# Fp16 halves for the values and probabilities of the second attention, with one more buffer for each pool and a new layout

## The chip, the cores and the metric

The kernel runs on one core of a Trainium2 chip, as one program from the input in DRAM to the output in DRAM. The time is in device microseconds. A core has five engines that run side by side and wait for each other through semaphores: TensorE (PE; its weight loads are listed apart as PEld), VectorE (DVE), ScalarE (ACT), GpSimd (POOL) and SyncE (SP), whose queue issues all transfers of this kernel. Each engine works through its instructions in order, so that an instruction that waits holds up everything behind it.

## What is computed

One block of a transformer on a sequence of 1024 positions of width 1024: a gated FFN at half weight, a mix of two attentions, a second FFN, and a last normalization.

```python
h = rmsnorm(x, ffn1_norm);  x = x + 0.5 * swiglu(h, w1, w3, w2)
h = rmsnorm(x, mix_norm);   x = x + token_mix(h, ...)
h = rmsnorm(x, ffn2_norm);  x = x + 0.5 * swiglu(h, ...)
return rmsnorm(x, final_norm)

# token_mix: proj = h @ w_in, split into the parts of both attentions
y_da  = diff_attention(q_da, k_da, v_da, ...)   # 8 heads: softmax(q1 k1) - lam * softmax(q2 k2), times v (128 wide)
# second attention, 16 heads in 2 groups of 8; a group shares keys and values of 64 columns
o_cmp = softmax(q @ kc) @ vc                    # kc, vc: 63 compressed blocks of keys and values
o_slc = softmax(qr @ ks, causal) @ vs           # top 16 of 16 blocks: every causal key
o_win = softmax(qr @ kw, last 512 keys) @ vw
y_ns  = g0 * o_cmp + g1 * o_slc + g2 * o_win
merged = sigmoid(g_a) * (y_da @ w_proj_da) + sigmoid(g_b) * (y_ns @ w_proj_nsa)
return merged @ w_out
```

Everything is in float32, and the kernel keeps near that accuracy by splitting an operand into a high and a low half and multiplying the halves apart.

## The kernel before

The span runs through these stages in turn: the first FFN (to about 700 us), projections and the compressed keys and values of the second attention (to about 970), the first attention (`da_phase`, with its own projections ahead, to about 1474), the second attention (`ns_phase`, 1474 to 2092), and the output products with the second FFN.

**The second attention.** Work goes head by head (`hd`, 16 of them, two of a pair for one `H`) and, within a head, over `m`, two blocks of 128 queries. `ns_scores` computes for each block the scores of the selected (`Ps`) and of the window branch (`Pw`): the matmuls on L886 (`S<-kt,qt`), the mask and maximum on DVE (L893), the exponential with its sum on ACT (L895), the normalization with the gate on POOL (L1052). `ns_pv` then multiplies probabilities and values of the block before. `tr_split` transposes up to four 128x128 pieces of probabilities into PSUM (L941, `tr`), and `split` makes two halves of them: ACT writes the high half `th` (L89), DVE the low half `tl` (L85). For each piece or pair of pieces two matmuls follow, with 128 or 256 columns, the values `vt` as the weights: `v` times `th` (L1098) and `v` times `tl` (L1099). The weights hold the values as high and low halves beside each other, 64 columns of each; `ns_fold` (L1107, L1108) adds the two halves of the result up. The compressed branch `pc` times `vc` opens each output tile (L1064). In between `fill.step` puts products of later stages (`gm`, L52 to L54, with weights `whi` and `wlo` from L1162 and L85) into the order of the engines.

**The first attention** has the same shape with its own lines (L963 to L965 for the three value products). Its `da_finish` copies the output (`ob`, L971) and squares it (`sq`, L973); `da_finish2` sums the squares with a matmul by ones (`tot`, L980), scales (`m`, L982), takes a reciprocal root (L155 to L160, on ACT and POOL), multiplies (L986) and splits into `yo` (L89, L85), which is stored (`syd`, L990).

**The values** of the second attention are made in `v_ns_unit`, in the stage of projections: a projection, transposes (`tr`, L671), the split into `vv` and a store per group into `s_v2` (`sv<-vv`, L675). `vv` has one buffer. `ns_load_values` reads them back as `vt`.

**What sets the order.** A scheduler places the instructions of each engine by priority, and a tile's buffers and address come from its pool in the order in which pools are opened. Pools of the second attention are laid over those of the first, so that a first write to a buffer waits for the last reader of what lay there before. SP issues its transfers in the order of its queue.

## Time and profile before

| | |
|---|---|
| median of 3 runs | 2930.38 us (2929.75 to 2931.03) |
| the profiled execution | 2929.13 us |
| its span, first to last instruction | 2927.3 us |
| mean granted clock of TensorE in the span | 0.989 |
| TensorE busy | 2813.9 us |
| DVE, ACT, POOL busy | 2003.0, 1364.6, 789.2 us |

The span is the time between the first and the last instruction of the core; 1.8 us of the profiled execution lie around it. Busy times are sums of an engine's instructions that count overlapping ones once. The granted clock is that of TensorE as a share of full speed. Times in the trace count from the span's start.

### The profile page before, as it was taken

To read this page: it belongs to the slowest core of one execution; us is meant where nothing else is said; L and a number is where in the kernel's file an instruction comes from. 1 tells how busy PE (TensorE), PEld (TensorE's weight loads), DVE (VectorE), ACT (ScalarE), POOL (GpSimd) and SP (SyncE) were. 2 spreads that over 40 slices of the span, in tenths; PEclk is the share of its full clock that TensorE was granted. 3 is DMA by queue.
4 is the path that set the end of the run, shared out by engine and by line. 5 is a ranking of instruction groups with operands and counts; after the bars stand their busy time and mean duration, and the time that the engine had idled before them with its cause. 6 is when DMAs were issued, how large, how long until landed. Compare 5 with 4: busy or idle time off the path is not lost. (4 is left out here: it accounts for less than half of the span.)

```text
span 2927.3 us, 40127 instructions
## 1 busy us (share of the span) xinstructions
PE 2813.9 (96%) x14276; PEld 2122.4 (73%) x14276; DVE 2003.0 (68%) x3347; ACT 1364.6 (47%) x2347; POOL 789.2 (27%) x701
## 2 busy tenths in 40 slices
PE   8999999999999899989989999999999999999998
PEld 6644447888788678778778988888888854444886
DVE  7876866666587467767767777777343876675666
ACT  7533424442333245445566666666332653343443
POOL 3133321000144123322233333333242414233001
PEclk9999999999999999999999999999999999999999
DMA  4355448655456545544432225222753246444854
GB/s 162 123 200 183 168 169 283 216 180 165 145 197 237 178 151 179 180 163 152 149 114 84 87 95 184 87 87 76 289 167 107 77 155 223 159 179 162 296 181 144
DMA packets 212713, 478.21 MB, mean 163 GB/s; under 512 B 20897, under 2 KB 39585, under 8 KB 212513
## 3 DMA queue, kind: packets, MB, share of 16 engines
q1 hardware_dynamic: 212512, 475.65, 47.6%
q8 instruction: 112, 1.84, 0.3%
q14 instruction: 89, 0.72, 0.1%
HBM read 313.56 MB, written 162.00 MB: 162 GB/s over the span
## 5 line engine op out<-in xcount | busy, mean ns | idle before, releaser
L405 PEld LDWEIGHTS <-w 128*128 128x128 f16 x3024 | 297.1, 99 | 381.9 <-issue 30.7
L52 PE MATMUL gm<-hi,whi 128*128 128x512 f32 x880 | 351.7, 400 | 4.2 <-ACT whi L89 1.8
L54 PE MATMUL gm<-hi,wlo 128*128 128x512 f32 x880 | 347.9, 396 | 1.1 <-DVE wlo L85 1.1
L53 PE MATMUL gm<-lo,whi 128*128 128x512 f32 x880 | 348.0, 395 | 0.0
L405 PE MATMUL Y<-tf,w 128*128 128x512 f16 x1296 | 296.3, 383 | 20.7 <-DVE u L443 16.9
L85 DVE TENSOR_TENSOR tl<-tr,th 128x512 fp32r<-128x512 f32 (+2 forms) x384 | 233.1, 619 | 86.3 <-ACT th L89 74.9
L886 PE MATMUL S<-kt,qt 128*128 128x320 f32 (+5 forms) x1152 | 264.0, 348 | 26.3 <-ACT Pt L895 9.6
L89 ACT ACTIVATE th<-tr 128x512 fp32r<-128x512 f32 (+2 forms) x384 | 201.5, 543 | 182.0 <-PE tr L941 172.6
L85 DVE TENSOR_TENSOR wlo<-st,whi 128x1024 fp32r<-128x1024 f32 x154 | 197.5, 1300 | 113.8 <-ACT whi L89 112.6
L893 DVE CUSTOM_DVE_ANT_0 S<-S,slab 128x896 f32<-128x896 f32 (+7 forms) x320 | 224.0, 710 | 50.3 <-PE S L886 45.1
L53 PE MATMUL acc<-wlo,whi 128*128 128x512 f32 (+1 forms) x628 | 244.1, 389 | 1.0 <-DVE wlo L85 1.0
L89 ACT ACTIVATE whi<-st 128x1024 fp32r<-128x1024 f32 x154 | 160.6, 1057 | 178.5 <-PE acc L54 107.3
L54 PE MATMUL acc<-whi,wlo 128*128 128x512 f32 (+1 forms) x628 | 242.8, 389 | 0.0
L52 PE MATMUL acc<-whi 128*128 128x512 f32 (+1 forms) x628 | 240.3, 387 | 0.0
L886 PEld LDWEIGHTS S<-kt,qt 128*128 128x128 f32 x1152 | 184.5, 190 | 43.6 <-ACT Pt L895 11.4
L1052 POOL TENSOR_SCALAR Ps<-Ps,l 128x384 f32<-128x384 f32 (+7 forms) x128 | 98.5, 770 | 404.9 <-DVE l L1050 236.9
L405 PE MATMUL X<-h,w 128*128 128x512 f16 x864 | 195.3, 379 | 0.5 <-ACT s L415 0.5
L52 PEld LDWEIGHTS gm<-hi,whi 128*128 128x128 f32 x880 | 168.0, 191 | 37.5 <-ACT whi L89 2.8
L54 PEld LDWEIGHTS gm<-hi,wlo 128*128 128x128 f32 x880 | 167.7, 191 | 37.4 <-DVE wlo L85 1.8
L53 PEld LDWEIGHTS gm<-lo,whi 128*128 128x128 f32 x880 | 168.0, 191 | 30.7
L85 DVE TENSOR_TENSOR wlo<-wst,whi 128x1024 fp32r<-128x1024 f32 x103 | 138.7, 1348 | 54.6 <-ACT whi L89 44.5
L1099 PE MATMUL o<-tl,vt 128*128 128x256 f32 (+1 forms) x608 | 159.3, 294 | 15.3 <-DVE tl L85 15.1
(320 smaller groups left out, 6123.0 us busy)
## 6 DMA issues: line engine op xcount, KB each, us to landing
wst<-in_win_dram SPq DMA_DIRECT2D x55, 512.0 KB
sw<-w2s SPq DMA_DIRECT2D x44, 512.0 KB
st<-sw SPq DMA_DIRECT2D x88, 256.0 KB
st<-saT SPq DMA_DIRECT2D x88, 256.0 KB
a<-in_f1w_dram SPq DMA_DIRECT2D x36, 512.0 KB
a<-in_f2w_dram SPq DMA_DIRECT2D x36, 512.0 KB
st<-saB SPq DMA_DIRECT2D x66, 256.0 KB
qt<-sq SPq DMA_DIRECT2D x128, 128.0 KB
```

Source lines behind the costliest of these rows:

```text
L52: first = nc.tensor.matmul(out, lhsT=w[0][:, wk], rhs=x[0], start=start, stop=False, skip_group_check=skip)
L53: nc.tensor.matmul(out, lhsT=w[0][:, wk], rhs=x[1], start=False, stop=False, skip_group_check=skip)
L54: nc.tensor.matmul(out, lhsT=w[1][:, wk], rhs=x[0], start=False, stop=stop, skip_group_check=skip)
L85: return nc.vector.tensor_tensor(out=lo, in0=src, in1=hi.bitcast(F32), op=ALU.subtract)
L89: nc.scalar.activation(out=hi, in_=src, func=AF.Copy)
L405: K.mark = nc.tensor.matmul(o, lhsT=w[:, a, m * h + k], rhs=x[k][:, b], start=start and k == 0 and i == 0, stop=k == h - 1 and i == 2, ski ...
L886: K.last = nc.tensor.matmul(S[:, o:o + n], lhsT=q, rhs=k[:, k0 + c:k0 + c + n], start=i == 0, stop=i == 1)
L893: nc.vector.tensor_tensor_reduce(out=sv, in0=sv, in1=mv, scale=-0.125, scalar=BIG, op0=ALU.add, op1=ALU.min, accum_out=nm)
L1052: nc.gpsimd.tensor_scalar(out=p[:, 0:n], in0=p[:, 0:n], scalar1=l[:, c:c + 1], scalar2=1.0, op0=ALU.mult, op1=ALU.mult)
L1099: nc.tensor.matmul(dst, lhsT=v, rhs=lo[:, b * P:(b + n) * P], start=False, stop=last, skip_group_check=True)
```

## The change

The values of the second attention and its transposed probabilities are held as two halves of fp16 instead of float32. For that `v_ns_unit` only copies the transposed values to `vraw` and adds up their squares; the new `ns_value_scale` derives one power of two from the sum, scales all values by it, splits them into fp16 halves and stores them. The probabilities are multiplied by 2^14 where POOL normalizes them, the compressed values by both factors, and `ns_fold` divides by both. `np`, the pool of probabilities, has 6 buffers instead of 5, and `nt`, that of `th` and `tl`, 4 instead of 3. The pools of `ns_phase` are opened in another order, with queries and `pc` in two pools of one buffer each; the first queries and the first `pc` are loaded ahead of `wslab`. `da_finish2` of the last head is placed under another priority.

```diff
@@ v_ns_unit
-        vv = K.mq.tile([P, 2, 4, 2, 64], F32R, tag="vv", name="vv")
+        nc.vector.tensor_copy(out=K.vraw[br][:, tb * 4:tb * 4 + 4], in_=tr)
+        jk = K.mq.tile([P, TB], BF16, tag="vj", name="vj")
+        nc.scalar.activation(out=jk, in_=tr.rearrange("p j d -> p (j d)"), func=AF.Square,
+                             accum_out=K.vss[:, br * 2 + tb:br * 2 + tb + 1])
+
+
+def ns_value_scale(K):
+    nc = K.nc
+    one = K.mq.tile([P, 1], F32, tag="vone", name="vone")
+    nc.vector.tensor_reduce(out=one, in_=K.vss, axis=AX.X, op=ALU.add)
+    tot = K.gm.tile([P, TB], F32, tag="gm", name="tot")[:, 0:1]
+    nc.tensor.matmul(tot, lhsT=K.ones, rhs=one, start=True, stop=True)
+    s, v = pow2_scale(K, K.cst, tot, 51)
+    K.vscale = K.cst.tile([P, 2], F32, name="vscale")
+    nc.vector.tensor_scalar(out=K.vscale[:, 0:1], in0=s, scalar1=P_NS, scalar2=None, op0=ALU.mult)
+    nc.vector.tensor_scalar(out=K.vscale[:, 1:2], in0=v, scalar1=1.0 / P_NS, scalar2=None, op0=ALU.mult)
+    for br in range(2):
         for g in range(2):
-            split(nc, vv[:, g, :, 0], vv[:, g, :, 1], tr[:, :, g * 64:(g + 1) * 64])
-            nc.sync.dma_start(out=K.s_v2[br][g][:, tb * 4:tb * 4 + 4],
-                              in_=vv[:, g].rearrange("p j a d -> p j (a d)").bitcast(F32))
+            src = K.vraw[br][:, :, g * 64:(g + 1) * 64]
+            t = K.mq.tile([P, 8, 2, 64], F16, tag="vv", name="vv")
+            nc.scalar.activation(out=t[:, :, 0], in_=src, func=AF.Copy, scale=s)
+            nc.vector.scalar_tensor_tensor(out=t[:, :, 1], in0=src, scalar=s, in1=t[:, :, 0], op0=ALU.mult, op1=ALU.subtract)
+            nc.sync.dma_start(out=K.s_v2[br][g], in_=t.rearrange("p j a d -> p j (a d)"))
...
@@ tr_split
-    hi = K.tp.tile([P, TB], F32R, tag="th", name="th")
-    lo = K.tp.tile([P, TB], F32R, tag="tl", name="tl")
-    split(nc, hi[:, 0:n], lo[:, 0:n], tr[:, 0:n])
+    dt = F16 if K.narrow else F32R
+    hi = K.tp.tile([P, TB], dt, tag="th", name="th")
+    lo = K.tp.tile([P, TB], dt, tag="tl", name="tl")
+    if K.narrow:
+        nc.scalar.activation(out=hi[:, 0:n], in_=tr[:, 0:n], func=AF.Copy)
+        nc.vector.tensor_tensor(out=lo[:, 0:n], in0=tr[:, 0:n], in1=hi[:, 0:n], op=ALU.subtract)
...
@@ ns_scores
+        p1 = K.pp.tile([P, 5 * P], F32, tag="P1", name="Pw")
         p0 = K.pp.tile([P, T], F32, tag="P0", name="Ps")
-        p1 = K.pp.tile([P, 5 * P], F32, tag="P1", name="Pw")
...
-            nc.gpsimd.tensor_scalar(out=p[:, 0:n], in0=p[:, 0:n], scalar1=l[:, c:c + 1], scalar2=1.0,
+            nc.gpsimd.tensor_scalar(out=p[:, 0:n], in0=p[:, 0:n], scalar1=l[:, c:c + 1], scalar2=P_NS,
@@ ns_pv
+            if hd + m == 0:
+                order_after(K, first, K.last)
@@ ns_fold
-    nc.scalar.activation(out=y[mine], in_=o[other], func=AF.Copy)
-    nc.vector.tensor_tensor(out=y[mine], in0=o[mine], in1=y[mine], op=ALU.add)
+    nc.scalar.activation(out=y[mine], in_=o[other], func=AF.Copy, scale=K.vscale[other, 1:2])
+    nc.vector.scalar_tensor_tensor(out=y[mine], in0=o[mine], scalar=K.vscale[mine, 1:2], in1=y[mine], op0=ALU.mult, op1=ALU.add)
@@ constants
-B_NP = 5
+B_NP = 6
-B_NT = 3
+B_NT = 4
@@ da_phase
-        da_finish2(K, *K.fin)
+        with K.tc.high_priority(offset=-100):
+            da_finish2(K, *K.fin)
@@ ns_phase
+        K.qp, K.pcp = [open_pool(K, ctx, "nq0", 1)], [open_pool(K, ctx, "npc0", 1)]
+        q0 = ns_queries(K, 0, 0)
+        pc0 = ns_compressed(K, 0, 0)
         K.wslab = open_pool(K, ctx, "wsl", 1).tile([P, 5 * P], F32, name="wslab")
         nc.sync.dma_start(out=K.wslab, in_=K.A["wslab"])
-        K.qp, K.kp, K.pcp = open_pool(K, ctx, "nq", 2), open_pool(K, ctx, "nk", 1), open_pool(K, ctx, "npc", B_NPC)
-        K.pp, K.sm, K.tp, K.op = (open_pool(K, ctx, "np", B_NP), open_pool(K, ctx, "nsm", 6), open_pool(K, ctx, "nt", B_NT),
+        K.kp = open_pool(K, ctx, "nk", 1)
+        K.pcp.append(open_pool(K, ctx, "npc1", 1))
+        K.qp.append(open_pool(K, ctx, "nq1", 1))
+        K.tp, K.sm, K.pp, K.op = (open_pool(K, ctx, "nt", B_NT), open_pool(K, ctx, "nsm", 6), open_pool(K, ctx, "np", B_NP),
```

Line numbers shift with the change: L886 becomes L909, L895 L918, L941 L964, L971 and L973 become L999 and L1001, L980 L1008, L1098 and L1099 become L1144 and L1145, L1162 becomes L1208.

On ACT, at the passage from the first attention to the second, before (the first rows are the last splits of the first attention, `ob` and `sq` its last finish, `Ps` and `Pw` the first exponentials of the second):

```order
L89 ACTIVATE th<-tr 128x384
L971 ACTIVATE ob<-o 128x512
L895 ACTIVATE Ps,l<-S,nm 128x128
L895 ACTIVATE Pw,l<-S,nm 128x128
L973 ACTIVATE sq<-ob 128x512
L1162 ACTIVATE whi<-wst 128x1024
L895 ACTIVATE Ps,l<-S,nm 128x256
L895 ACTIVATE Pw,l<-S,nm 128x256
L895 ACTIVATE Ps,l<-S,nm 128x384
L155 ACTIVATE yr<-m 128x512
```

and after:

```order
L89 ACTIVATE th<-tr 128x384
L999 ACTIVATE ob<-o 128x512
L1001 ACTIVATE sq<-ob 128x512
L155 ACTIVATE yr<-m 128x512
L156 ACTIVATE yr<-yr 128x512
L157 ACTIVATE zr<-yr 128x512
L89 ACTIVATE yo<-ob 128x512
L918 ACTIVATE Ps,l<-S,nm 128x128
L918 ACTIVATE Pw,l<-S,nm 128x128
L918 ACTIVATE Ps,l<-S,nm 128x256
```

The steps of the finish, from `sq` to `yo`, have moved ahead of the first exponential.

On TensorE at the same place, from the last value product of the first attention on, before:

```order
L965 MATMUL o<-th,vt 128x128
L886 MATMUL S<-kt,qt 128x256 x2
L52 MATMUL gm<-hi,whi 128x512
L53 MATMUL gm<-lo,whi 128x512
L54 MATMUL gm<-hi,wlo 128x512
L52 MATMUL gm<-hi,whi 128x512
L53 MATMUL gm<-lo,whi 128x512
L54 MATMUL gm<-hi,wlo 128x512
L886 MATMUL S<-kt,qt 128x384 x2
L980 MATMUL tot<-sq,ones 128x512
```

and after:

```order
L993 MATMUL o<-th,vt 128x128
L1008 MATMUL tot<-sq,ones 128x512
L909 MATMUL S<-kt,qt 128x256 x2
L52 MATMUL gm<-hi,whi 128x512
L53 MATMUL gm<-lo,whi 128x512
L54 MATMUL gm<-hi,wlo 128x512
```

The finish's product by ones, `tot`, now stands first behind the value products.

On ACT in the stage of projections, behind the activation `gt` of the compressed keys, before (`vv` are the last two splits of the values, `kc` and `kbh` the compressed keys, `rh` a rotated projection, `whi` weights):

```order
L796 ACTIVATE gt<-gt 126x256
L89 ACTIVATE vv<-tr 128x4x64 x2
L809 ACTIVATE kc<-kcp 128x128
L812 ACTIVATE kbh<-kc 32x2x64 x4
L809 ACTIVATE kc<-kcp 128x128
L89 ACTIVATE whi<-wst 128x1024
L89 ACTIVATE rh<-m_6073 128x1024
```

and after:

```order
L817 ACTIVATE gt<-gt 126x256
L692 ACTIVATE vv<-vraw_5578,sc 128x8x64 x2
L692 ACTIVATE vv<-vraw_5579,sc 128x8x64 x2
L830 ACTIVATE kc<-kcp 128x128
L833 ACTIVATE kbh<-kc 32x2x64 x4
L830 ACTIVATE kc<-kcp 128x128
L89 ACTIVATE rh<-m_6092 128x1024
L89 ACTIVATE whi<-wst 128x1024
```

All four writes of `vv` stand here in a row now, and `rh` stands ahead of `whi`.

## Rows read from the trace of the kernel before

**Rows 1.** The page's busy times of the two busiest engines: busy us, share of the span, instructions.

```profile
PE 2813.9 (96%) x14276; PEld 2122.4 (73%) x14276; DVE 2003.0 (68%) x3347; ACT 1364.6 (47%) x2347; POOL 789.2 (27%) x701
```

**Rows 2.** Busy times by stretch of the span: window, its length, then the busy us (and instructions) of PE, PEld, DVE, ACT and POOL, the mean granted clock of TensorE, the share of the DMA engines, GB/s.

```profile
1453.00:1474.00 21.00, 16.77 (x90) 12.98 (x89) 10.17 (x18) 9.11 (x16) 4.85 (x4) 0.84 0.28 104
1474.00:1491.00 17.00, 15.60 (x77) 12.79 (x78) 13.51 (x49) 12.26 (x36) 9.43 (x16) 1.00 0.65 238
1491.00:1502.00 11.00, 3.44 (x19) 2.81 (x18) 3.19 (x7) 2.14 (x5) 1.47 (x2) 0.68 0.27 95
1540.00:2040.00 500.00, 490.62 (x3247) 444.33 (x3246) 379.61 (x985) 327.94 (x765) 154.39 (x217) 1.00 0.30 101
```

**Rows 3.** The waits in 1540 to 2040: engine, tile and line, what it waited for, then us in total, times, longest.

```profile
PEld o L1099 <- DVE tl L85: 10.1, 21, 0.8
PE o L1099 <- DVE tl L85: 5.8, 16, 0.6
```

**Rows 4.** Groups of instructions by line and shape, 1474 to 2092: count, then busy us and mean ns of one, then idle time before them. L1099 has the same counts as L1098.

```profile
L1098 PE MATMUL o<-th,vt 128*128 128x256 f32 x448 | 129.7, 302 | 0.4 <-ACT th L89 0.2
L1098 PE MATMUL o<-th,vt 128*128 128x128 f32 x160 | 37.0, 235 | 0.1
```

**Rows 5.** Timeline of TensorE in the second attention: start us, duration us, engine, line, what, count.

```profile
1691.04 0.22 PE L1098 MATMUL o<-th,vt 128*128 128x128 f32 x1
1691.21 0.27 PE L1098 MATMUL o<-th,vt 128*128 128x128 f32 x1
1695.35 0.28 PE L1098 MATMUL o<-th,vt 128*128 128x256 f32 x1
1695.82 0.28 PE L1098 MATMUL o<-th,vt 128*128 128x256 f32 x1
```

**Rows 6.** Timeline of TensorE in the first FFN: eleven matmuls in one row.

```profile
159.18 2.54 PE L405 MATMUL X<-h,w 128*128 128x512 f16 x11
```

**Rows 7.** The page's groups of instructions, two of the FFN: count, then busy us and mean ns of one, then idle time before them.

```profile
L405 PEld LDWEIGHTS <-w 128*128 128x128 f16 x3024 | 297.1, 99 | 381.9 <-issue 30.7
L405 PE MATMUL Y<-tf,w 128*128 128x512 f16 x1296 | 296.3, 383 | 20.7 <-DVE u L443 16.9
```

**Rows 8.** Groups by line: count, then the shortest, median and longest duration in ns, first and last start, forms.

```profile
L89 ACT ACTIVATE th<-tr x384: 372/588/616, 1046.1 to 2087.1; 128x512 fp32r<-128x512 f32 x128, 128x384 fp32r<-128x384 f32 x48, 128x256 fp32r<-128x256 f32 x16
L94 ACT ACTIVATE tf<-x x16: 613/624/632, 66.5 to 91.4; 128x512 f16<-128x512 f32 x16
L95 DVE TENSOR_TENSOR h<-x,h x12: 674/679/1784, 64.5 to 84.0; 128x512 f16<-128x512 f32 x12
L1098 PEld LDWEIGHTS o<-th,vt x608: 186/188/338, 1491.3 to 2088.1; 128*128 128x128 f32 x152
```

**Rows 9.** Timeline of TensorE and DVE at the handover: start us, duration us, engine, line, what, count, and in brackets the idle time before it and what ended that.

```profile
1455.43 0.30 PE L886 MATMUL S<-kt,qt 128*128 128x128 f32 x1 [1.23 <-DMA qt<-sqn]
1456.65 1.28 DVE L929 SCALAR_TENSOR_TENSOR Pt<-Pt,l 128x1024 f32<-128x1024 f32 x1 [1.02 <-POOL Pt L927]
1457.96 1.44 PE L886 MATMUL S<-kt,qt 128*128 128x128 f32 x5 [2.24 <-DMA qt<-sqn]
1462.18 2.11 PE L941 MATMUL tr<-ident,Pt 128*128 128x128 f32 x8
1475.00 0.51 PE L886 MATMUL S<-kt,qt 128*128 128x256 f32 x2 [1.04 <-ACT Ps L895]
1499.86 1.62 DVE L85 TENSOR_TENSOR tl<-tr,th 128x384 fp32r<-128x384 f32 x3 [7.18 <-DMA syd<-yo]
1500.48 0.58 PE L1099 MATMUL o<-tl,vt 128*128 128x256 f32 x1 [6.68 <-DVE tl L85]
```

**Rows 10.** Groups by line of the first attention's finish, columns as in rows 8.

```profile
L980 PE MATMUL tot<-sq,ones x32: 590/592/1061, 1064.0 to 1477.5; 128*128 128x512 f32 x32
L157 ACT ACTIVATE zr<-yr x16: 615/632/668, 1067.4 to 1481.8; 128x512 f32<-128x512 f32 x16
L158 POOL TENSOR_TENSOR zr<-zr,m x16: 1279/1294/2282, 1068.3 to 1483.2; 128x512 f32<-128x512 f32 x16
L986 DVE SCALAR_TENSOR_TENSOR ob<-ob,hgain,yr x16: 736/744/1196, 1078.3 to 1488.8; 128x512 f32<-128x512 f32 x16
```

**Rows 11.** Timeline of SP, ACT, DVE and TensorE in the stage of projections, columns as in rows 9; a row of SP is the issue of a transfer.

```profile
721.79 0.33 SPq L675 DMA_DIRECT2D sv<-vv  x1
725.19 0.37 ACT L89 ACTIVATE vv<-tr 128x256 fp32r<-128x256 f32 x1
735.80 2.12 DVE L771 TENSOR_TENSOR bf<-bt,pos 128x504 f32<-128x504 f32 x2
744.73 0.28 ACT L809 ACTIVATE kc<-kcp 128x128 f32<-128x128 f32 x1 [5.80 <-PE kcp L807]
746.67 1.06 ACT L89 ACTIVATE whi<-wst 128x1024 fp32r<-128x1024 f32 x1
749.17 0.42 SPq L143 DMA_DIRECT2D wst<-in_win_dram  x1
754.04 1.06 ACT L89 ACTIVATE whi<-wst 128x1024 fp32r<-128x1024 f32 x1 [1.44 <-DMA wst<-in_win_dram]
755.15 0.50 PE L52 MATMUL gm<-hi,whi 128*128 128x512 f32 x1 [1.76 <-ACT whi L89]
```

More of the change, by code (lines that the diff above doesn't have):

```diff
@@ L1028, in ns_load_values, with ns_compressed, ns_queries @@
             pool, tag = (K.mp, "m42") if g and br else (K.kp, f"v{g}{br}")
-            t = pool.tile([P, 8, P], F32R, tag=tag, name="vt")
-            K.nc.sync.dma_start(out=t.bitcast(F32), in_=K.s_v2[br][g])
+            t = pool.tile([P, 8, P], F16, tag=tag, name="vt")
+            K.nc.sync.dma_start(out=t, in_=K.s_v2[br][g])
             K.nv[g, br] = t
+def ns_compressed(K, pr, H):
+    pc = K.pcp[H].tile([P, 2, TB], F32R, tag="pc", name="pc")
+    K.nc.sync.dma_start(out=pc.bitcast(F32), in_=K.s_pc[pr][H])
+    return pc
+def ns_queries(K, hd, H):
+    qt = []
+    for z in range(2):
+        t = K.qp[hd % 2].tile([P, TB], F32R, tag=f"q{z}", name="qt")
+        K.nc.sync.dma_start(out=t.bitcast(F32), in_=K.s_qns[hd // 4][z:z + 2, :, hd % 4, :, H * TB:(H + 1) * TB]
+                            .rearrange("h a d t -> (h a) d t"))
+        qt.append(t)
+    return qt
 def ns_scores(K, hd, m, qt, g, step):
@@ L1063, in ns_pv @@
         for hl in range(2):
[L1064 to L1065 removed]
+            first = nc.tensor.matmul(o, lhsT=K.vc[:, g, par].rearrange("p a d -> p (a d)"), rhs=pc[:, hl], start=hl == 0,
+                                     stop=False, skip_group_check=True)
+            if hd + m == 0:
+                order_after(K, first, K.last)
     work = []
@@ L1264, in prelim @@
         K.Gc = c0.tile([P, 8, 16], F32, name="Gc")
+        K.vraw = [c0.tile([P, 8, P], F32, name=f"vraw{i}") for i in range(2)]
+        K.vss = c0.tile([P, 4], F32, name="vss")
         nc.vector.memset(K.kbh.bitcast(F32), 0.0)
@@ L1408, in ns_phase @@
                 for H in range(2):
-                    pc = K.pcp.tile([P, 2, TB], F32R, tag="pc", name="pc")
-                    nc.sync.dma_start(out=pc.bitcast(F32), in_=K.s_pc[pr][H])
+                    pc = ns_compressed(K, pr, H) if pr + H else pc0
                     y = K.op.tile([P, TB], F32, tag="y", name="y")
@@ L1413, in ns_phase @@
                         hd = pr * 2 + par
-                        qt = []
-                        for z in range(2):
-                            t = K.qp.tile([P, TB], F32R, tag=f"q{z}", name="qt")
-                            nc.sync.dma_start(out=t.bitcast(F32), in_=K.s_qns[hd // 4][z:z + 2, :, hd % 4, :, H * TB:(H + 1) * TB]
-                                              .rearrange("h a d t -> (h a) d t"))
-                            qt.append(t)
+                        qt = ns_queries(K, hd, H) if hd + H else q0
                         for m in (2 * H, 2 * H + 1):
@@ L1504, in body @@
         K.s_v = [[dr.tile([P, 8, P], F32, name=f"sv{h}_{i}") for i in range(2)] for h in range(8)]
-        K.s_v2 = [[dr.tile([P, 8, P], F32, name=f"sv2{h}_{i}") for i in range(2)] for h in range(2)]
+        K.s_v2 = [[dr.tile([P, 8, P], F16, name=f"sv2{h}_{i}") for i in range(2)] for h in range(2)]
         K.s_raw = [dr.tile([P, T], F32, name=f"sraw{h}") for h in range(2)]
```

15 lines of the change are left out of this document (9 added, 6 removed).

## The prediction, made before the changed kernel ran

> **What bounds the kernel now.** I read the busy shares first [rows 1]: TensorE is busy for 96% of the span and the next engine for 68%, so a microsecond counts only if TensorE works less or waits less. The table by stretch [rows 2] says where each is to be had. In the body of the second attention (1540 to 2040) TensorE is busy 490.62 of 500.00 us: 9.4 us are idle, so the body gets much shorter only through shorter matmuls. At the handover from the first attention it is the other way round: 1491 to 1502 holds 3.44 us of matmuls in 11.00, and 1453 to 1474 holds 16.77 in 21.00 at a mean granted clock of 0.84. The waits of the body [rows 3] name who is late there: the low halves `tl`, 10.1 us ahead of the weight loads and 5.8 ahead of the matmuls of the same instructions. Last, I read the handover and the preparation of the values event by event [rows 9, 11].
>
> **Part 1: the value products in fp16.** 608 matmuls on L1098 and as many on L1099 become fp16. By form [rows 4] 448 of each line have 256 columns and 160 have 128. What counts is the distance from start to start in an unbroken train, since TensorE's durations overlap. In float32 [rows 5] four steps of 256 columns go from 1695.35 to 1695.82, 117.5 ns each, and two of 128 columns from 1691.04 to 1691.21, 85 ns each. No fp16 product of these sizes is in the trace. The nearest row is the FFN's train of eleven 512-column fp16 matmuls, 2.54 us [rows 6]: less the 0.38 us of the last [rows 7], ten steps of 216 ns. Halved, that gives 108 ns for 256 columns, and halved again 54 for 128. So the upper bound is 896 x 9.5 ns = 8.5 us and 320 x 31 ns = 9.9 us, together 18.4 us; the lower bound is nothing, if short fp16 products keep the float32 pitch. A loss has no row behind it. I take 13: the fp16 row is the nearer one, but a product that comes sooner finds `tl` late more often [rows 3], so some of the gain turns into waiting.
> The Trainium skill, page "TensorE: Matmul & The Clock Gate", section "Back-to-back issue gap", speaks against the second half of this: it gives about 81 ns for each 128-column matmul in a stream with its weight load, and by it the 128-column part would be some 1 us, an estimate, and the term about 9. The same section has 131 ns for 512 columns, where the row here has 216; no row here has 128 fp16 columns.
>
> Writing fp16 costs nothing more by the rows [rows 8]: ACT's fp16 copy of 512 columns takes 624 ns where `th` takes 588 at the median, DVE's fp16 remainder 679. What hides a difference is that both engines have time between splits. Were that cover gone, 36 ns on 384 splits would be 14 us of ACT. The added scale of the fold and POOL's other constant ride on instructions that are there already.
>
> **Part 2: the handover.** Three things move, all on TensorE's path.
> (a) The first queries lie in other memory, and their two loads now stand ahead of `wslab` on SP. Before, TensorE waits 1.23 and 2.24 us for them, and the eight transposes of `Pt` begin only at 1462.18. `Pt` itself was ready at 1456.65 + 1.28 = 1457.93 [rows 9]. So the gain lies between nothing and 4.2 us; I take 4.
> (b) In the new ACT order the whole last finish stands ahead of the second attention's first exponential, and TensorE's score buffers wait for that exponential. The finish is one chain of 512-column steps: ACT's `ob`, `sq`, three of the root and `yo`, six at 0.63 = 3.8 us; `tot` on TensorE 0.59; two on DVE at 0.74 = 1.5; on POOL two at 1.29 and one that I put at half of that, 3.2 [rows 10]. With some 0.3 for the hops that is 9.4 us from the end of the last value product, about 1474. The exponential then begins at 1483.4 and TensorE resumes at some 1483.9 instead of 1475.00 [rows 9], 8.9 later. The `tot` product falls into this gap: +8.4. After an idle stretch of this kind the trace shows the lower level of the clock: in 1491 to 1502, which holds a wait of 6.68 us, the mean granted clock is 0.68 [rows 2, 9]. I add 2 us for the matmuls that run at it.
> (c) The wait of 6.68 us for `tl` goes. `tl` was held for 7.18 us by the store of `yo`, over which its buffer lay [rows 9]; in the new layout no `tl` lies there. That is -6.7 and, with the slow clock behind it, another -2.
> Together -4 + 10.4 - 8.7 = about -2. Bounds: -8 if much of the finish is covered by matmuls that are still queued, +5 if (a) gives nothing and the clock stays down longer.
>
> **Part 3: more buffers.** `np` goes from 5 to 6 and `nt` from 3 to 4. Beside part 2 they could shorten TensorE's idle time of 1474 to 1491 and 1540 to 2040, 1.4 + 9.4 = 10.8 us [rows 2]; but `tl` is late by DVE's place in the order, which hardly moves. I take -1, with -11 and +5 as ends (the latter is the 5.8 us of [rows 3] once more).
>
> **Part 4: preparing the values.** Eight small writes, splits and stores become four copies, four squares, a reduction, and then four larger writes through one buffer, `vv`. In the new ACT order these four stand in a row, ahead of `kc`, `kbh`, `rh` and `whi`, and each but the first waits until the store before it has landed. One turn is ACT 0.62, DVE 0.68 [rows 8], a hop of 0.1, and the store, x from issue to landing: 1.4 + x. The first split stands behind DVE's two `bf` steps, which end at 735.80 + 2.12 = 737.92 [rows 11], so it is stored at about 738.7. The fourth ACT write then ends near 738.7 + 2 x 1.4 + 0.7 + 3x = 742.2 + 3x; after `kc`, `kbh` and `kc` (1.9 us, from 744.73 to 746.67) and `rh`, which is as large as `whi` (1.06), `whi` begins at 745.2 + 3x instead of 746.67 [rows 11]: 3x - 1.5 late. The lateness reaches TensorE in full. `whi` and its `wlo` free a staging buffer, the load of the next weights is issued behind that at 749.17, `whi` of 754.04 waits for that load, and TensorE at 755.15 for that `whi`, already 1.76 us [rows 11].
> For x: at 238 GB/s, the core's rate in 1474 to 1491 [rows 2], 256 KB take 1.1 us, the lower bound; a store issued at 721.79 had landed before the write at 725.19, so 3.4 is the upper [rows 11]. I take the middle, 2.3: 3 x 2.3 - 1.5 = 5.4. The new `tot` product waits for its reduction, which I put at two DVE steps, 0.9. Sum +6, bounds +3 to +10.
>
> **Sum.** -13 - 2 - 1 + 6 = -10. From the profiled execution's 2929.13 us this gives 2919.1; the median of the runs is 1.25 higher, so **2920 us**. With parts 1, 2 and 4 at bounds all the one way it would be -18 - 8 - 1 + 3 = -24, 2906; with part 1 at 8 and part 2 at nothing, 2927. The forecast's own range is 2908 to 2928.
>
> **Rivals.**
> A, the other side: the store chain is long, because the stores share the queue with weight loads. Part 4 costs 3x - 0.6 with the `tot` wait, all else gives -16. At x = 4.9, what the weight load of 512 KB takes from 749.17 to its use at 754.04 [rows 11], the sum is -2 (2928); at x = 8 it is +7 (2938). It decides from x = 5.5. Against it: the store above, landed within 3.4.
> B, the weight loads are on the path. A float32 load takes 188 ns [rows 8] and an fp16 one 99 [rows 7]; if the path were loads, 1216 x 89 ns = 108 us would go: 2812. Against it: loads of 188 ns belong to matmuls that start every 117.5 ns, so they overlap already [rows 5, 8].
> The Trainium skill, the same page, section "Weight-path perf modes — Fast Weight Load (FWL) and DoubleRow", says that 128 weights of a type other than FP32 load in about half the time. The two rows on loads agree; the overlap in the sentence before says that it isn't what TensorE waits for.
> C, the deeper buffers remove TensorE's idle time in the body altogether: 10 us more than I took, 2910, and 2902 where part 1 comes out at its upper end and part 4 at its lower. For it: the idle time names `tl`, whose buffers grow. Against it: `tl` is named as late work of DVE, not as a full buffer.
> D, the products don't get shorter: fp16 at 256 and 128 columns steps like float32, 13 us back, 2933. For it: at 256 columns float32 is within 9% of half the fp16 pitch already. Against it: nothing in float32's 85 ns at 128 columns is explained by the columns alone.
>
> **How the numbers follow.** A measurement of this kernel tells some 0.2%, 5.9 us, from no change. The forecast has 0.60, A 0.17, C 0.13, D 0.06, B 0.04. Faster ends at 2924.5: of the forecast 0.55 lies below it and 0.05 above. Faster: 0.55 + 0.13 + 0.04 = 0.72. Same: 0.04, D 0.06 and 0.10 of A (x from 3.6 to 7.5), 0.20. Slower: 0.01 and 0.07 of A, 0.08. The range 2900 to 2934 takes in C, D and the near half of A; it leaves out B, the far half of A and the tails of the forecast and of C, some 0.17.
>
> **What would show it.** Part 1 right: steps of 108 ns in trains of `o<-th,vt` with 256 columns, and 54 to 60 with 128. Part 2: no wait for `qt` at 1455, an idle stretch of 8 to 9 us before the first exponential, and no `tl` that waits for a store. Part 4: three gaps of ACT ahead of the `vv` writes, ended by stores, and a TensorE wait of 5 to 8 us for `whi` where 1.76 stood. The prediction is wrong if a short fp16 product has a floor above 80 ns, if the finish is covered, or if one of the reordered steps makes TensorE wait where the trace of before shows no wait at all.

## The result and the profile after

The changed kernel takes 2908.32 us (median of 6 runs, 2905.20 to 2913.63) against 2930.10 us before (6 runs, 2924.36 to 2931.03). The ratio is 0.993 with a 95% interval of 0.9917 to 0.9943: 17 to 24 us faster. Forecast were 2920 us and a range of 2900 to 2934: the direction and the range held, but the gain is 22 us and not 10. The profiled execution has a span of 2905.0 us (before 2927.3), and from it come the numbers that follow.

The page's rows on busy times, which answer to [rows 1]:

```profile
span 2905.0 us, 40199 instructions
PE 2791.6 (96%) x14278; PEld 2056.3 (71%) x14278; DVE 1997.1 (69%) x3356; ACT 1371.3 (47%) x2351; POOL 785.8 (27%) x701
```

TensorE's busy time fell by 22.3 us, which is the whole gain of the span: over the whole it waits as long as before and works less. Three marks that stand in both programs, with as many matmuls between them, show where. They are the first value product of the first attention, the first product of the compressed branch for the second pair of heads, and the last value product of the second attention (timeline of TensorE, start and duration in us). Before:

```profile
1048.10 0.28 PE L963 MATMUL o<-th,vt 128*128 128x256 f32 x1
1574.63 0.62 PE L1064 MATMUL o<-pc,vc 128*128 128x512 f32 x2
2088.29 0.28 PE L1099 MATMUL o<-tl,vt 128*128 128x128 f32 x1
```

After:

```profile
1048.91 0.28 PE L991 MATMUL o<-th,vt 128*128 128x256 f32 x1
1570.69 0.50 PE L1108 MATMUL o<-pc,vc 128*128 128x512 f32 x1
2065.87 0.22 PE L1145 MATMUL o<-tl,vt 128*128 128x128 f16 x1
```

The first stretch, call it U, holds the first attention, the handover and the second attention's first pair of heads: 526.5 us before, 521.8 after. The second, B, is the body, the other seven pairs: 513.7 and 495.2 (513.66 and 495.18). What comes behind, T, up to the last matmul, is 826.7 in both. So 18.5 us come from the body and 4.7 from the stretch with the handover, while the mark ahead of both is 0.8 us late.

**The products.** Trains of TensorE after, against [rows 5] (256 columns first, then 128):

```profile
1836.34 0.28 PE L1144 MATMUL o<-th,vt 128*128 128x256 f16 x1
1837.22 0.27 PE L1144 MATMUL o<-th,vt 128*128 128x256 f16 x1
...
1557.05 0.22 PE L1145 MATMUL o<-tl,vt 128*128 128x128 f16 x1
1557.22 0.39 PE L964 MATMUL tr<-ident,Ps 128*128 128x128 f32 x2
```

Eight steps of 256 columns take 0.88 us, 110 ns each; three of 128 columns take 0.17 us, 57 ns each. Over the whole stage the median step from start to start is 119.5 ns before and 109 after with 256 columns, and a pair of 128 columns takes 171 ns before (59 and 112) and 112 after. By these medians the products save 896 x 10.5 ns and 160 x 59 ns, 18.8 us.

**The waits in the body** (1540 to 2040, TensorE, as [rows 3]): the products found `tl` late less often, not more. Other waits grew: that of the compressed branch for the fold's `y` was 0.6 us before.

```profile
PE o L1145 <- DVE tl L970: 4.2, 13, 0.5
PE o L1108 <- DVE y L1154: 2.8, 5, 0.8
```

Over B as a whole TensorE's busy time fell from 503.4 to 483.6 us, and its idle time rose from 10.3 to 11.6.

**The handover** (timeline of TensorE, as [rows 9]):

```profile
1455.83 1.02 PE L909 MATMUL S<-kt,qt 128*128 128x128 f32 x5
...
1472.19 1.13 PE L1008 MATMUL tot<-sq,ones 128*128 128x512 f32 x2 [1.35 <-ACT sq L1001]
1481.33 0.80 PE L909 MATMUL S<-kt,qt 128*128 128x256 f32 x2 [8.01 <-ACT Ps L918]
1481.92 0.63 PE L52 MATMUL gm<-hi,whi 128*128 128x512 f32 x1
1482.35 0.63 PE L53 MATMUL gm<-lo,whi 128*128 128x512 f32 x1
...
1485.12 0.39 PE L52 MATMUL gm<-hi,whi 128*128 128x512 f32 x1
1485.35 0.39 PE L53 MATMUL gm<-lo,whi 128*128 128x512 f32 x1
```

The wait for the first queries is gone (no bracket at 1455.83), the gap ahead of the first exponential has come (8.01 us), and behind it `gm` steps by 0.43 us until some 1484.4 and by 0.23 later: three microseconds at the lower level of the clock (1.2 GHz), which cost 1.5.

The end of the first attention cuts U in two. Busy times from its last value product to the end of U, before and after (columns as in [rows 2]):

```profile
1473.72:1574.63 100.91, 90.75 (x562) 80.88 (x561) 72.49 (x199) 61.47 (x150) 33.44 (x48) 0.95 0.29 104
```

```profile
1470.60:1570.69 100.09, 87.88 (x562) 70.81 (x561) 68.81 (x191) 61.21 (x149) 32.32 (x49) 0.95 0.28 97
```

This part is 0.8 us shorter, and the first attention, where the wait for the queries was, 3.9 (425.6 to 421.7).

**The values** (timeline of ACT, then of TensorE, as [rows 11]):

```profile
735.78 0.71 ACT L692 ACTIVATE vv<-vraw,sc 128x512 f16<-128x512 f32 x1
740.97 0.72 ACT L692 ACTIVATE vv<-vraw,sc 128x512 f16<-128x512 f32 x1 [4.48 <-DMA sv<-vv]
744.58 0.72 ACT L692 ACTIVATE vv<-vraw,sc 128x512 f16<-128x512 f32 x1 [2.89 <-DMA sv<-vv]
748.24 0.72 ACT L692 ACTIVATE vv<-vraw,sc 128x512 f16<-128x512 f32 x1 [2.94 <-DMA sv<-vv]
...
751.75 1.04 ACT L89 ACTIVATE whi<-wst 128x1024 fp32r<-128x1024 f32 x1
```

```profile
754.30 0.39 PE L803 MATMUL hid<-wlo,bh 128*126 128x256 f32 x1 [0.95 <-DVE wlo L85]
...
759.20 0.50 PE L52 MATMUL gm<-hi,whi 128*128 128x512 f32 x1 [3.21 <-ACT whi L89]
```

One turn of `vv`, from one write to the next, takes 3.61 to 3.66 us, so x is 2.2 (forecast 2.3), and `whi` is 5.1 us late (forecast 5.4). TensorE's wait for it grew from 1.76 to 3.21 us, less than the 5 to 8 that were named as the sign.

### The profile page after: what moved, and what is told of

It is laid out like the page before. It is cut to its first block, busy times and chain, and to the rows that moved or that the text cites. A ratio compares the mean times of both kernels' runs of the same rounds, so it can differ in the third digit from the quotient of the medians.

```text
span 2905.0 us, 40199 instructions
## 1 busy us (share of the span) xinstructions
PE 2791.6 (96%) x14278; PEld 2056.3 (71%) x14278; DVE 1997.1 (69%) x3356; ACT 1371.3 (47%) x2351; POOL 785.8 (27%) x701
## 5 line engine op out<-in xcount | busy, mean ns | idle before, releaser
L909 PE MATMUL S<-kt,qt 128*128 128x320 f32 (+5 forms) x1152 | 268.9, 352 | 27.0 <-ACT Pt L918 11.1
L909 PEld LDWEIGHTS S<-kt,qt 128*128 128x128 f32 x1152 | 183.1, 190 | 43.9 <-ACT Pt L918 13.1
L970 DVE TENSOR_TENSOR tl<-tr,th 128x512 f16<-128x512 f32 (+2 forms) x304 | 183.8, 615 | 43.8 <-ACT th L969 42.5
L969 ACT ACTIVATE th<-tr 128x512 f16<-128x512 f32 (+2 forms) x304 | 159.4, 540 | 79.6 <-PE tr L964 65.8
L521 POOL TENSOR_TENSOR u<-u,u 128x512 f32<-128x512 f32 x36 | 52.0, 1444 | 344.3 <-DVE sa L102 162.1
```

What stands on the lines that cost most here:

```text
L521: nc.gpsimd.tensor_tensor(out=a, in0=a, in1=b, op=ALU.mult)
L909: K.last = nc.tensor.matmul(S[:, o:o + n], lhsT=q, rhs=k[:, k0 + c:k0 + c + n], start=i == 0, stop=i == 1)
L969: nc.scalar.activation(out=hi[:, 0:n], in_=tr[:, 0:n], func=AF.Copy)
L970: nc.vector.tensor_tensor(out=lo[:, 0:n], in0=tr[:, 0:n], in1=hi[:, 0:n], op=ALU.subtract)
```

## The experiments

Each is the changed kernel or the kernel before with one thing undone, added or replaced. The table gives the median, the ratio to the kernel before on the same chip with its 95% interval, and the stretches U, B and T of the profiled execution, from the starts of the same marks. The runs come from several chips, on which the kernel before takes 2927.5 to 2930.1 us, so that the ratios compare better than the medians. Executions of one kernel differ by up to 9.5 us, so that parts of 3 us are told from the stretches; B agrees within 0.3 us over the five kernels with 6 and 4 buffers, U within 1.4.

| kernel | median us | ratio (95%) | U | B | T |
|---|---|---|---|---|---|
| before (float32, 5 and 3 buffers) | 2930.1 | 1 | 526.5 | 513.7 | 826.7 |
| changed (fp16, 6 and 4) | 2908.3 | 0.993 (0.9917 to 0.9943) | 521.8 | 495.2 | 826.7 |
| e1 changed, four vv | 2908.2 | 0.9928 (0.9916 to 0.994) | 522.5 | 495.5 | 828.4 |
| e2 changed, nk behind np | 2908.0 | 0.9926 (0.9914 to 0.9939) | 523.2 | 495.4 | 827.3 |
| e3 fp16 alone, 5 and 3 | 2907.5 | 0.9926 (0.9914 to 0.9938) | 514.3 | 498.0 | 834.1 |
| e4 layout alone, float32, 5 and 3 | 2930.4 | 1.0004 (0.9995 to 1.0013) | 529.1 | 513.9 | 826.9 |
| e5 changed, pools nt, nk, nsm, np first | 2909.3 | 0.993 (0.9917 to 0.9943) | 523.0 | 495.4 | 825.1 |
| e6 changed, 5 and 3 | 2906.0 | 0.9922 (0.9908 to 0.9937) | 513.9 | 497.9 | 831.9 |
| e7 as e3, four vv | 2901.9 | 0.991 (0.9895 to 0.9925) | 513.6 | 498.1 | 833.7 |
| e8 as e5, four vv | 2907.8 | 0.9927 (0.9915 to 0.9939) | 523.0 | 495.5 | 827.7 |
| e9 as e7, 5 and 4 | 2897.4 | 0.9895 (0.988 to 0.991) | 510.5 | 500.4 | 825.6 |
| e10 changed, 5 and 4, four vv | 2901.1 | 0.9907 (0.9894 to 0.9921) | 515.0 | 500.1 | 824.8 |
| e11 changed, 6 and 3 | 2914.2 | 0.9953 (0.9941 to 0.9966) | 521.3 | 499.7 | 831.7 |
| e12 changed, 5 and 4, four vv, old order behind the first queries | 2897.8 | 0.9883 (0.9866 to 0.9899) | 511.0 | 501.7 | 826.7 |

**e1: is the chain of value stores worth its 6 us?**

```diff
-            t = K.mq.tile([P, 8, 2, 64], F16, tag="vv", name="vv")
+            t = K.mq.tile([P, 8, 2, 64], F16, tag=("vv", "vv1", "vv2", "vt")[br * 2 + g], name="vv")
```

> The changed kernel with four buffers for vv instead of one, nothing else. Theory of the prediction (part 4): the four value writes wait for no store any more (three waits of 4.48, 2.89 and 2.94 us on ACT in the changed kernel), kc comes when its product is done, whi begins near 747 instead of 751.75, and TensorE's wait for whi at 759 falls from about 3.5 to about 1.8 us; the stretch to there gets some 4 to 6 us shorter. In the changed kernel about 3 of the 6.6 us lost there were made up before the first attention, so the whole gains 3 to 6 us (2902 to 2905). Rival: the lateness is made up in full further on, and the whole time is the same within 2 us although the waits are gone.

The waits are gone and the gain is not there. ACT's four writes stand in one row, `whi` begins 2.7 us sooner, and the first score product of the first attention starts at 972.43 instead of 975.05. ACT, and then TensorE:

```profile
735.74 2.55 ACT L692 ACTIVATE vv<-vraw,sc 128x512 f16<-128x512 f32 x4
...
749.02 1.04 ACT L89 ACTIVATE whi<-wst 128x1024 fp32r<-128x1024 f32 x1
```

```profile
972.43 0.30 PE L909 MATMUL S<-kt,qt 128*128 128x128 f32 x1 [0.68 <-DMA kt<-sk]
```

Of the 2.6 us, 1.6 are left at the first value product (1047.3 against 1048.9), and the whole time doesn't show them. The rival holds for the whole time. Part of the reason stands at the first attention's first score, in the kernel before and in the changed one:

```profile
973.89 0.45 PE L886 MATMUL S<-kt,qt 128*128 128x128 f32 x1 [3.88 <-issue]
```

```profile
975.05 0.30 PE L909 MATMUL S<-kt,qt 128*128 128x128 f32 x1 [0.31 <-DMA kt<-sk]
```

Before, TensorE stood idle there for 3.88 us; in the changed kernel it comes 4.7 us later (last `gm` at 974.36 instead of 969.63) and waits 0.31, for the keys. The lateness of the values is paid out of a wait that was there already, and 1.2 us of it remain. The profile doesn't name what the wait of before was for; that it was the keys too is read from the row after.

**e2: does the gap ahead of the first exponential cost its 8 us?**

```diff
-        K.kp = open_pool(K, ctx, "nk", 1)
         K.pcp.append(open_pool(K, ctx, "npc1", 1))
...
+        K.kp = open_pool(K, ctx, "nk", 1)
+        K.op = open_pool(K, ctx, "no", B_NO)
```

> The changed kernel with one pool opened later: nk (keys and values) behind np (probabilities), so that the second Ps buffer no longer lies over ob and sq of the first attention; buffer counts as in the changed kernel. The order of ACT then has the first exponentials ahead of sq and the rest of the finish, as before the change. Theory of the prediction (part 2b): TensorE's gap of 8.60 us at 1472.7 shrinks to about 1 us, the half-speed matmuls behind it go, and the whole gains 8 to 10 us (2898 to 2900). Rival: the finish has only been moved, its store of yo is again waited for by something that lies over it (as tl before the change, 6.68 us), and the whole gains less than 3 us.

The gap went, and a wait of 9.10 us came in its place: the rival, with another carrier than it named. TensorE, then SP:

```profile
1499.92 0.39 PE L1144 MATMUL o<-th,vt 128*128 128x256 f16 x1 [9.10 <-DMA vt<-sv]
```

```profile
1491.10 2.27 SPq L1058 DMA_DIRECT2D vt<-sv  x3
```

The loads of the values are now issued right behind the finish's last store (1489.52), 21 us later than in the changed kernel (1469.93). By the order of the pools the values lie where the finish keeps its tiles; the addresses themselves stand in no trace.

**e3 and e4: which half of the change carries the gain?** e3 takes out the buffers, the layout, the order of the two P tiles, the early loads and the priority; e4 takes out fp16, with 5 and 3 buffers since 6 and 4 don't fit in float32.

```diff
# e3, against the changed kernel
-B_NP = 6
+B_NP = 5
-B_NT = 4
+B_NT = 3
...
+        qp, K.kp, pcp = open_pool(K, ctx, "nq", 2), open_pool(K, ctx, "nk", 1), open_pool(K, ctx, "npc", 2)
+        K.qp, K.pcp = [qp, qp], [pcp, pcp]
+        K.pp, K.sm, K.tp, K.op = (open_pool(K, ctx, "np", B_NP), open_pool(K, ctx, "nsm", 6), open_pool(K, ctx, "nt", B_NT),
+                                  open_pool(K, ctx, "no", B_NO))
```

> Only the fp16 part of the change: values, probabilities and scale as in the changed kernel, but 5 and 3 buffers, the pools in the old order, the old order of the two P tiles and of the loads, and no priority for the last finish. Theory with part 1 at its upper end (steps of 109 and 56 ns in the changed kernel, which by medians is 18.8 us): -19, and +6 less the 3 made up for the values, so 16 us faster than before (2914), with the waits for qt at 1455 and for tl at 1500 still there. Rival: the products give the 13 us that I took, and about a third of the gain is owed to buffers and layout: 2918 to 2922.

> The other part alone: the kernel before with the new order of pools, first loads and P tiles, and the priority of the last finish, but in float32 and with 5 and 3 buffers (6 and 4 don't fit in float32). Theory of the prediction (part 2): the waits for qt go (-4), the gap before the first exponential comes (+8.4 and 2 for the clock), the wait of tl for the store goes (-8.7): 0 to -4 us against before. Rival: if layout is what carried the unexpected 11 us, this is 8 us or more faster than before.

fp16 alone gives the whole gain, 22 us, and layout alone gives nothing (1.0004). In e4 the queries' wait and the store's are gone, and the gap with the slow clock has come, as in the changed kernel; U is 2.6 us longer than before, where the theory had 0 to 4 less. The part behind the first attention is 2.4 us longer (theory +1.7). What fell short is the early queries: the first attention takes as long as before (425.7 us), among others because TensorE waits 1.89 us for `th` at 1462.68. TensorE in e4:

```profile
1482.95 0.80 PE L886 MATMUL S<-kt,qt 128*128 128x256 f32 x2 [8.01 <-ACT Ps L895]
```

In e3, U is 12.2 us shorter, although its layout has the old order. All the waits of TensorE above 1 us between 1440 and 1540 are those for the queries:

```profile
PE S L909 <- DMA qt<-sqn: 3.8, 2, 2.2
```

The wait of 6.68 us for `tl` ([rows 9]) is gone without the new layout, and fp16 is all that e3 changes. The likely reason is that fp16 tiles take half the room, so that the same order of pools puts `tl` elsewhere. The new layout then buys the queries' 3.8 us for a gap of 8.

**e5 and e6: the gap taken out in two other ways.** e5 opens the pools in another order (its diff is that of e2 with the lines in the order its expectation names), e6 has the buffers of before.

> The changed kernel with its pools in the order nt, nk, nsm, np, npc1, nq1, no: buffer counts unchanged, the first exponentials stand ahead of the finish of the first attention, and the loads of the values stay where they were on SP, so that the wait of the run with nk behind np (TensorE 9.1 us for vt) should not come. Theory: the gap of 8.60 us before the first exponential is a true loss, and without it and its slow clock the stretch from the last value product of the first attention to the last of the second falls from 595.3 to about 586 us and the whole to about 2899. Rival: the stretch is held by something else (ACT, DVE or POOL fall behind as they work the finish off among the scores), the gap's time comes back as waits for th, tl or Ps, and the stretch stays above 592 and the whole within 3 us of the changed kernel.

> The changed kernel with 5 and 3 buffers instead of 6 and 4, its pools in its own order. With one Ps buffer less the first exponentials come ahead of the finish. Theory (part 3: deeper buffers are worth next to nothing, the gap is worth 9): the stretch of the second attention takes about 586 us as in the run before this one, and the waits for tl in the body stay near 6 us. Rival: the deeper buffers are what kept the tl waits from growing when the products became shorter; then the waits for tl and th on TensorE grow by 5 us or more and eat the gain of the missing gap.

e5 is the rival again: the first exponentials come early, but now TensorE waits for `y`, for the next queries and for `th`. ACT's `y` waits for the store of `yo`, over which it seems to lie. SP waits 9.1 us to issue that store, and the loads of the next queries stand right behind it. The waits of TensorE from 1469 to 1540, then those of ACT there and of SP (1469 to 1500):

```profile
PE o L1108 <- DVE y L1154: 4.6, 1, 4.6
PE S L909 <- DMA qt<-sqn: 4.2, 2, 2.2
PE o L1144 <- ACT th L969: 2.2, 2, 1.8
```

```profile
ACT y L1153 <- DMA syd<-yo: 2.2, 1, 2.2
```

```profile
SPq L1018 <- ACT yo L89: 9.1, 1, 9.1
```

With 6 and 4 buffers U is 521.8 to 523.2 in all five kernels, whichever tile pays: `Ps` (changed, e1), `vt` (e2), `y` and the queries (e5, e8). The single waits differ, and their sum hardly does: over U, TensorE is idle for 38.5 to 40.0 us in these five, and for 30.1 in e3. e6, with less memory in use, has U at 513.9 in the new layout as e3 has 514.3 in the old one (32.7 us idle; 3.7 of them for queries again). That is the theory's 8 us. But the whole is only 2906.0, because B is 2.7 and T 5.2 us longer.

**Why T is longer.** Behind the second attention, for each block of output columns, TensorE multiplies the attention's result `yl` by weights (`pj`). SP loads the gates `sg` from `smx`; ACT, POOL and DVE merge them with `pj`, and ACT writes the high half `mh` of the merged output, which the next product `po` needs. In e3, e6, e7 and e11, the four fp16 kernels with three `th` and `tl` buffers, TensorE waits there for `whi` (1.2 to 1.4 us) and for `mh` (0.6 to 1.0), and T is 831.7 to 834.1; in the eight with four it doesn't, and T is 824.8 to 828.4.

**e7 and e8: the same with four `vv` buffers.** e7 is e3 with e1's edit, e8 is e5 with it.

> The run with the fp16 part alone, with four buffers for vv. It is a second look at that version, whose second attention took 583.6 us (changed kernel 595.3) while its output products and second FFN took 5 us longer than in all other profiles. Theory A: that loss behind the second attention is chance (waits for DVE in the FFN that differ from execution to execution): then the stretch behind the first po product takes 739 to 741 us here and the whole comes to about 2902. Theory B: it follows from this layout (weights of pj and po later): then it takes 745 again and the whole is 2905 to 2908. The vv buffers by themselves give about 3 us up to the first scores, of which the wait for the keys there takes most.

> Both repairs: pools in the order nt, nk, nsm, np, npc1, nq1, no, and four buffers for vv. Theory: 9 from the handover and 1 to 3 from the values, 2897 to 2899, the fastest of all. Rival as for the two parts: within 3 us of the changed kernel (2905 to 2908).

For e7 theory B holds in the profile (T 833.7 as in e3), and the median is nearer to A's (2901.9); the two can't be reconciled from one profile. e8 gives nothing beside e5. What TensorE waits for in e7, and ACT's and SP's instructions ahead of it:

```profile
2082.73 0.50 PE L52 MATMUL pj<-yl,whi 128*128 128x512 f32 x1 [1.27 <-ACT whi L89]
```

```profile
2077.40 1.06 ACT L1493 ACTIVATE sg<-sg 128x1024 f32<-128x1024 f32 x1 [4.67 <-DMA sg<-smx]
2081.10 0.63 ACT L89 ACTIVATE mh<-sg 128x512 fp32r<-128x512 f32 x1 [2.64 <-POOL sg L1498]
2081.64 1.99 ACT L89 ACTIVATE whi<-wst 128x1024 fp32r<-128x1024 f32 x2
```

```profile
2034.63 0.33 SPq L143 DMA_DIRECT2D wst<-in_wns_dram  x1
...
2055.44 0.32 SPq L770 DMA_DIRECT2D smx<-vt  x1
2056.11 1.26 SPq L143 DMA_DIRECT2D wst<-in_wns_dram  x1
2061.23 1.27 SPq L1492 DMA_DIRECT2D sg<-smx  x3
...
2074.26 10.01 SPq L1513 DMA_DIRECT2D xx<-sx  x15
...
2086.03 1.01 SPq L143 DMA_DIRECT2D wst<-in_wns_dram  x2
```

`whi` is late because ACT is: it waits for a gate's load and for POOL, and `whi` stands behind `mh` in its order. The chain starts at the last store of `smx`, for which the loads of `sg` wait. That store is issued 3.9 us ahead of the last value product here (3.5 to 3.9 in the four kernels with three buffers), 7.5 in the changed kernel and 9.8 in e9. Why the third or fourth buffer moves it isn't shown.

In the second FFN one more wait shows in e3, e6 and e7: TensorE waits 2.0 to 2.5 us for DVE's `u`, where it waits 1.0 in e1 and e9 and not at all in the changed kernel, and the seven or eight products behind it step by 0.43 us instead of 0.22, at the lower level of the clock; together that is some 4 us. In e7, first behind that wait and then without one:

```profile
2627.69 4.44 PE L405 MATMUL Y<-tf,w 128*128 128x512 f16 x12 [1.99 <-DVE u L443]
...
2633.58 2.75 PE L405 MATMUL Y<-tf,w 128*128 128x512 f16 x12
```

**e9 to e11: which of the two counts does what?** Only the two numbers differ (and, in e9 and e10, e1's edit stands with them).

```diff
# e9 against e7, e10 against the changed kernel, e11 against the changed kernel
-B_NT = 3
+B_NT = 4
...
-B_NP = 6
+B_NP = 5
...
-B_NT = 4
+B_NT = 3
```

> The fp16 part alone with the pools in the old order and four buffers for vv, as two runs before, but 5 and 4 buffers instead of 5 and 3. With a fourth th and tl buffer both loads of the next weights (wst) stand ahead of the sixteen xx loads on SP at the end of the second attention; with three, one of them stands behind. Theory: the waits of TensorE for whi and mh behind the second attention (1.6 and 1.3 us in all three fp16 kernels with 5 and 3 buffers) come from that order on SP; they go here, the stretch from the last value product to the first po product is 87.2 us again instead of 88.9, the stretch behind it about 740 instead of 743 to 745, while the second attention keeps its 584 us: 2895 to 2899 in all. Rival: the time is held elsewhere and comes back as other waits: 2901 to 2908.

> The changed kernel with 5 and 4 buffers instead of 6 and 4 and four buffers for vv. The first exponentials stand ahead of the finish, the first queries come early, and nothing of the second attention's first tiles but the sixth pair of probabilities is gone. Theory: from the first value product of the first attention to the last of the second 1012 us, as in all fp16 kernels with 5 probability buffers (1018 in all with 6), and no waits for whi and mh behind: 2895 to 2899. Rival: the fourth th and tl buffer makes the body slow and not the sixth probability buffer: 1018 and 2903 to 2906.

> The changed kernel with 6 and 3 buffers. Its ACT order at the handover is that of the changed kernel (the finish ahead of the first exponential), its SP order at the end that of the kernels with three th and tl buffers (one of the two wst loads behind the xx loads). Theory: a gap of some 8 us and 1018 us for both attentions, and the waits for whi and mh behind them: the worst of both, 2911 to 2914. Rival: the sixth buffer isn't what costs: 1012 us, 2906 to 2908.

e9 takes the time that the theory forecast, but not for its reason: no wait of TensorE is left between the last value product and 2160, and T is 825.6. The theory put the waits down to a load of weights (`wst`) that stands behind the sixteen `xx` loads, which hold SP for ten microseconds. But of the eight loads of these weights four stand ahead of `xx` in every kernel, and in e7 the loads behind `xx` are issued at 2086.03, when ACT had already written the `whi` that TensorE waited for (begun at 2081.64). The weights were there; ACT wasn't.

With a ratio of 0.9895 e9 is 10 us faster than the changed kernel, and the intervals don't touch. e11 is the worst of both, as forecast: the gap of 8.0 us, the waits for `whi` and `mh`, 2914.2 us. e10 came out between: T is short, but U + B is 1015.1, neither 1012 nor 1018. A sum that is fixed by the number of probability buffers alone, as I had it, is too simple. Taking back one count alone makes the body longer than taking back both: B is 500.1 in e10 and 499.7 in e11, 497.9 in e6 and 495.2 in the changed kernel.

**e12: the early queries without the gap.** It is the changed kernel with e1's edit, 5 probability buffers and another order of pools, so that against e9 it has the early queries and also the changed order of the two P tiles and the priority of the last finish:

```diff
+        K.qp.append(open_pool(K, ctx, "nq1", 1))
         K.kp = open_pool(K, ctx, "nk", 1)
         K.pcp.append(open_pool(K, ctx, "npc1", 1))
-        K.qp.append(open_pool(K, ctx, "nq1", 1))
-        K.tp, K.sm, K.pp, K.op = (open_pool(K, ctx, "nt", B_NT), open_pool(K, ctx, "nsm", 6), open_pool(K, ctx, "np", B_NP),
-                                  open_pool(K, ctx, "no", B_NO))
+        K.pp = open_pool(K, ctx, "np", B_NP)
+        K.sm = open_pool(K, ctx, "nsm", 6)
+        K.tp = open_pool(K, ctx, "nt", B_NT)
+        K.op = open_pool(K, ctx, "no", B_NO)
```

> The fp16 kernel with 5 and 4 buffers and four buffers for vv, and of the new layout the early first queries: nq0 and npc0 opened first and loaded ahead of wslab, then wslab, nq1, nk, npc1, np, nsm, nt, no, that is the old order of the rest. In the run with the old order throughout TensorE waits 3.5 us for the first queries at the handover, in the changed kernel 0. Theory: that wait goes and nothing of the second attention's first tiles lies over the last finish, so the finish stays among the scores: 3 to 4 us faster than that run, 2893 to 2895. Rival: what comes behind the queries was waiting for the probabilities of the first attention's last block in any case, or another first tile now lies over the finish: within 1.5 us of that run or slower.

By the stretches the rival holds: the wait for the queries is gone and U is 0.5 us longer than in e9, not 3 to 4 shorter. In its place TensorE waits 1.5 us for `th` and 1.2 for `sq` in the first attention's last block. The whole time can't decide it: the ratio is 0.0012 lower than that of e9, some 3.5 us, and the intervals overlap.

## Why the prediction was right, and where it was off

- **What bounds the kernel**: right. In B TensorE's busy time fell by 19.8 us and the stretch by 18.5, and B in the five kernels with 6 and 4 buffers does not move whatever happens at the handover.
- **Part 1, the step that was mis-sized.** The working gave 18.4 us and I took 13, "some of it turns into waiting". The steps are 109 and 56 ns (108 and 54 in the working) and the medians give 18.8. The discount was too large. In the changed kernel 1.3 us of B turned into waiting, and not for `tl`, whose wait fell from 5.8 to 4.2 us in the body. With the buffers of before (e6) TensorE's idle time in B is 3.3 us longer than before and B 15.8 shorter, so that part 1 alone comes to about 18 us; the deeper buffers gave another 2.7 back. The busy time of B fell by 3.3 us more than the medians give for it (seven eighths of 18.8, 16.5); they don't cover the passages between products and transposes, and where these 3.3 us lie isn't shown. The Trainium skill's page "TensorE: Matmul & The Clock Gate", section "Back-to-back issue gap", has two figures for 128 columns: 81 ns in a stream and, by its formula for a single gap, N/2.4 + 2.5 = 56. These rows agree with the formula, at 256 columns too (109), and not with the 81. By the 81 the term would be 9.8, an estimate like the "about 9" of the working, which is too low.
- **Part 2**: the sum was right (-2 forecast). U is 4.7 us shorter, of which the first pair's fp16 products, one eighth of 18.8, are some 2.4; so about 2.3 are left for the handover. The split agrees too: the first attention, with the queries (a), is 3.9 shorter (-4 forecast), and the rest of U, less 2.4 for the products, 1.6 longer (+10.4 - 8.7 forecast). In that rest 8.0 us of gap were seen where 8.4 were forecast, and 1.5 us of slow clock where I had 2. Two things stand against calling it shown: the same layout in float32 (e4) gave +2.6 and not -2, and fp16 alone (e3) loses the 6.68 us without any new layout. The end of that wait was taken as a merit of the new layout.
- **Part 4**: x was 2.2 (2.3 forecast), `whi` 5.1 us late (5.4), and the waits on ACT stood where they were expected; TensorE's wait for `whi` was 3.21 us and not 5 to 8. And "the lateness reaches TensorE in full" was wrong beyond the stage: the first attention's first score had 3.88 us of idle time ahead of it, and of the 4.7 us by which the stage's last product is later, 1.2 were left at that score. I had put +6 into the sum, and 0.8 reached the first mark.
- **The 12 us between forecast and result** are thus about 7 from parts 1 and 3 and 5 from part 4. B and the first pair together are 20.9 shorter where 14 were forecast; by e6 some 5 of these 7 belong to part 1 and 2 to part 3. Both errors lie the same way, so that nothing cancelled.
- **The rivals.** A: x is not long. B: TensorE's weight loads fell to 98 ns each, and in the second attention they are busy 67 us less (the windows below: the PEld column falls from 535.38 to 468.27 us, the length by 19.4), so that the loads did not set the pace. C, idle time gone from the body through the deeper buffers, named 2910, and 2908 was measured, nearer than the forecast. But its mechanism isn't there: TensorE's idle time in B did not go, it rose from 10.3 to 11.6 us, and the deeper buffers are worth 2.7 us by e6, where C had 10.8. D fell.

Busy times from the last value product of the first attention to the last of the second, columns as in [rows 2], before and after:

```profile
1473.90:2088.50 614.60, 594.14 (x3867) 535.38 (x3867) 451.13 (x1154) 389.77 (x901) 188.52 (x259) 0.99 0.33 112
```

```profile
1470.80:2066.00 595.20, 571.37 (x3867) 468.27 (x3867) 444.23 (x1148) 393.37 (x901) 188.63 (x259) 0.99 0.34 115
```

What stays open: why the waits in U add up to nearly the same sum, whichever of the first tiles waits; why the number of `th` and `tl` buffers moves the last store of `smx`, and why DVE's `u` is later in e3, e6 and e7; and how much the four `vv` buffers are worth in e9, which wasn't run without them. That the priority of the last finish matters was not tried.

## What to carry to other kernels

A wait at a passage between two phases can be the price of an address, or of a place in the DMA queue: a tile of the new phase that lies over the last tiles of the old one, or a load that stands behind their last store, comes only when the old phase is done. Here other orders of the pools passed that price on to another tile. U came down to 510.5 to 515.0 us only in the six kernels that have fp16 and 5 probability buffers, in the old order of pools as in the new. So less memory may be worth more at such a passage than a new layout.

Where one engine is the bound, the gain of shorter instructions is what their train shows, and lateness put ahead of a wait that is already there costs only what exceeds that wait. A deeper buffer should be judged by what it moves in the order of the other queues too: one more pair of `th` and `tl` buffers went here with gates that came earlier on ACT, a stage later. And a wait is traced back from the instruction that was late: here the late `whi` led to ACT's own order, and not to the loads of the weights, which had been issued long before.

## What the runs showed of the hardware

fp16 products of 128 columns with a weight load each step by 56 ns (57 in the train above) where float32 pairs alternate 59 and 112, and their 98 ns loads hide as the 188 ns ones do. The gap of 8.0 us on TensorE was followed by a stretch at the lower level of the clock, 1.2 GHz (`gm` steps of 0.43 instead of 0.23 us), of some 3 us in the changed kernel, 5 in e1 and 6 in e4.
